# Second layer of a two-layer diffusion backbone: values scaled by one factor from norm bounds, gate loads spread over the score units, order fitted anew

## The chip, the cores and the metric

The kernel runs on one core of a Trainium2 chip. The metric is the device time of one execution in microseconds, as the median of several runs. The engines are TensorE (PE; its weight loads are listed as PEld), VectorE (DVE), ScalarE (ACT), GpSimd (POOL) and SyncE (SP), whose queue issues nearly all DMAs here.

## The reference

512 latent tokens and 256 context tokens of width 1024 pass through two layers: differential attention, then grouped-query attention (8 query heads, 2 key/value heads of width 128). Only the second layer's latent output is returned, and its context tokens are needed for keys and values alone.

```
shift, scale, gate = adaln(c, ada_w[i], ada_b[i])          # silu(c) @ w + b, split in three
h = rms_norm(x, pre_g[i]) * (1.0 + scale) + shift
...
q, k, v, z = jnp.split(p, [...], axis=-1)                  # p = h @ w_in
q = rms_norm(q, qk_g[0]); k = rms_norm(k, qk_g[1])         # then rotary positions on latent tokens
...
p = jax.nn.softmax(s, axis=-1)
o = einsum(p, v)
y = (o * silu(z)) @ w_out[i]
x = x + gate * rms_norm(y, post_g[i])
```

All inputs are float32.

## The kernel before, in words

**Precision.** A float32 product is made of three matmuls on split operands (a high part and the rest): hi*hi, hi*lo, lo*hi. Weights are loaded into a two-buffer tile `raw`, cast on ACT to `whi` (L240) and subtracted on DVE or POOL to `wlo` (L234). The class `WStream` does this in a fixed order as its slots come free.

**Second layer.** After the first layer's output projection the second layer's input `h1` is made, 256 tokens at a time, by `h1_tr` (L1342 on): transposes on TensorE, four scalings with shift per call (L1353; the first `HFD` of the four on DVE, the others on ACT; `HFD` is 4) and a split. Then comes the key/value stage: the list `KV` orders six projections (`k`, tokens m), the last two `h1_tr` calls (`t`) and the key transposes (`c`). Each projection fills a PSUM bank with 256 columns of keys and 256 of values. PSUM has four such banks in rotation (`trp` takes one briefly, `pj` holds one until `close`) and two double banks for scores.

**Values before.** Each value tile is copied to `vr` (L1450). When all six are there, they are squared to bf16 (L1457), summed over tokens on TensorE with a matrix of ones (L1459), and `col_scale` (L247 on) makes of each column's sum a power of two: Ln, Exp, and a mask on the exponent bits. Two transposes (L1465) and `col_back` make the factors that undo the scale. Then the values are multiplied by their columns' factors (L1469), cast to fp16 (L1470), and the rest is subtracted (L1471): `vp`, high and low.

**Score units.** 32 steps, four per head with 128 queries each (`s1_units`): scores, row maximum, Exp, reciprocal, a scaled copy to fp16 (`fp`, L258) and its rest (L1563). A DMA transpose on the SP queue (`turn`, L245) writes them to `ft`. Per half head (two units) 18 fp16 matmuls (`pv1_steps`, `pv_f16`, L179) multiply `ft` by the values.

**The gate.** The second layer's gate vector is computed on DVE from 512 KB slices of `ada_w`: `gate1_load` (L1601) loads a slice into `gw` (two buffers), `gate1_part` adds two products (L1614, L1616). After four slices `gate1_finish` sums over the partitions on TensorE (`colsum`), and adds the bias and multiplies by the post-norm gain (L1626, L1628). These two rows are loaded in `gate1_finish` itself, broadcast to all partitions (256 KB each), into the weight stream's `raw` tile (L1624, L1625). Loads go out after score units 1 to 8, and the two halves are finished after units 9 and 14 (`GFIN`).

**What sets the order.** `flow` is a planner: each step has a cost, lags behind other steps and a due time on a model clock. It emits the due step or, where none is due, a piece of filler work (`FILL1`: query and gate projections). `TS` spaces the score units, `LA` and `LT` are the lags of value matmuls behind scores, `SLAG1`, `QLAG` and `QTR` are other lags, `HOT1` and one row of `JT` per head are priorities and offsets. A scheduler then orders each engine's queue by these priorities.

**Near the end** `last_half` (L1630 on) multiplies the last head by its SiLU gate on the engine named by `EGL`; `subln_last` does the same in the first layer.

Of the kernel before, what the change touches and what calls it, by code (L numbers as in the profile page):

```python
# [9 lines left out]
F32 = mybir.dt.float32  # L10
# [24 lines left out]
ATT = 15.15  # L35
ACCN = (0, 1, 2, 2, 4, 0, 5, 4)
ACD = 0.71
FILL1 = (('q', 1), ('z', 2), ('z', 0), ('q', 2), ('q', 3), ('z', 1), ('z', 4), ('z', 5), ('z', 3), ('z', 6), ('z', 7))
HOT0 = (4643, 2452, 770, 3759)
HOT1 = (1948, 4101, 2904, 5806, 2112, 918)  # L40
WARM = 2019
AGB = 10
PRE = 19.12
TS = 8.22
HFD = 4
KVE = (0, 0, 1, 0)
KV = (('t', 1), ('k', 0), ('k', 2), ('k', 1), ('t', 0), ('c', 1), ('k', 3), ('c', 0), ('k', 4), ('c', 3), ('c', 2), ('k', 5))
SPL = 4.55
GAP0 = 7.06
DL0 = (0.86, 0.0, 0.73, 2.42, 2.07, 3.84, -1.78, 5.34)  # L50
# [2 lines left out]
NWARM = 16  # L53
XLATE = 1
WX = (1, 1)
LA = (9.42, 7.7)
LT = (1.27, 1.09)
AHEAD = 3
SLAG = (4.63, 0.61)
SLAG1 = 2.73  # L60
AT1 = 7.65
EGL = 'p'
EXS = 'pvvvvv'
EHF = ('vvvvvvpv', 'pvvvvvvv')
EHL = ('vvvvvvvv', 'pppppppp')
# [15 lines left out]
EG1 = 'a'  # L81
EGA = "v"
RL = 4.34
LM = (4.63, 10.96)
AB = 3
FTB = 6
JT = (((-0.86, -0.75, -0.84, -18, -0.26, 0.57), (0.1, -0.44, 0.02, 160, 0.11, -1.79), (0.07, -0.16, -0.26, -299, 1.1, 0.1), (-0.21, 0.31, -1.04, 23, 0.94, 0.71), (-0.21, -0.39, 0.3, 92, 2.85, -0.8), (-0.63, -0.11, 0.88, 16, -0.68, -3.71), (2.06, -0.05, 1.19, 296, -2.27, -0.21), (-0.02, 0.45, 1.73, -49, -0.48, 0.83)), ((-3.15, 0.21, -0.44, -128, 2.28, 0.65), (1.34, -0.8, -0.13, -164, 0, 0.55), (-2.3, -0.59, -1.0, -170, -0.88, -0.01), (0.16, -0.46, 0, -31, -0.58, -0.59), (0.54, -0.33, 0.91, 452, -1.34, -0.68), (0.65, -0.93, -2.71, 0, -0.85, -0.67), (0, -0.48, -0.44, 1330, 0, -1.3), (-0.03, 0.1, -1.26, -97, -0.6, 0.06)))


def f32(ap):  # L90
# [4 lines left out]
def tile_backbone(  # L95
# [90 lines left out]
    nc.vector.tensor_copy(ones_r, ones)  # L186
    eps = con.tile([P, 1], F32, name="eps")
    nc.vector.memset(eps, EPS)
    tiny = con.tile([P, 2], F32, name="tiny")
    nc.vector.memset(tiny[:, 0:1], 1e-30)  # L190
    nc.vector.memset(tiny[:, 1:2], 14.0 * math.log(2.0))
    mhalf = con.tile([P, 2], F32, name="mhalf")
    nc.vector.memset(mhalf, -0.5)

# [49 lines left out]
    def turn(dst, src):  # L244
        nc.sync.dma_start(dst, src, transpose=True)  # L245

    def col_scale(c, ss):  # L247
        nc.scalar.activation(c, ss, AF.Ln, bias=tiny[:, 0:1])  # L248
        nc.scalar.activation(c, c, AF.Exp, scale=-0.5, bias=tiny[:, 1:2])
        nc.vector.tensor_scalar(c.bitcast(I32), c.bitcast(I32), EXPO, None, ALU.bitwise_and)  # L250
# [1124 lines left out]
    with tc.tile_pool(name="t1", bufs=1, side="right") as t1p:  # L1375
# [7 lines left out]

        kh = t1p.tile([P, 2, T], F32R, name="kh")
        kl = t1p.tile([P, 2, T], F32R, name="kl")
        vr = t1p.tile([P, NT, 256], F32, name="vr")
        vp = t1p.tile([P, 2, NT, 256], F16, name="vp")
        vback = t1p.tile([P, 2], F32, name="vback")
        ones_b = t1p.tile([P, P], BF, name="ones_b")
        nc.vector.tensor_copy(ones_b, ones)  # L1390

        def rope_tok(dst, src, t):
            n = 2
# [44 lines left out]

        for what, m in KV:
            if what == "t":  # L1440
                hot(h1_tr, 2, m)
            elif what == "c":
                k_tr(*ktr.pop(0))
            else:
                o = pj(512)
                run(proj_tok(o, wkv, m))
                if late:
                    k_rope(*late.pop())
                late.append((m, o, head_rstd(o)))
                nc.scalar.copy(vr[:, m, :], o[:, 256:])  # L1450
        k_rope(*late.pop())
        while ktr:
            k_tr(*ktr.pop(0))
        vsq = vp[:, 1].bitcast(BF)
        ss = pj(256)
        for a in (0, 3):
            nc.scalar.activation(vsq[:, a:a + 3], vr[:, a:a + 3], AF.Square)  # L1457
        for m in range(NT):
            nc.tensor.matmul(ss, ones_b, vsq[:, m, :], start=m == 0, stop=m == NT - 1)  # L1459
        vc = t1p.tile([P, 256], F32, tag="qt", name=nm("vc"), bufs=9)  # L1460
        col_scale(vc, ss)
        close(ss)
        tr = trp()
        for g in range(2):
            nc.tensor.transpose(tr[:, g * P:(g + 1) * P], vc[:, g * P:(g + 1) * P], ident)  # L1465
        col_back(vback, tr[:, 0:256:P], 2.0 ** -16)
        for a in (0, 3):
            v = vr[:, a:a + 3]
            nc.vector.tensor_tensor(v, v, vc.unsqueeze(1).to_broadcast([P, 3, 256]), ALU.mult)  # L1469
            nc.scalar.copy(vp[:, 0, a:a + 3], v)  # L1470
            nc.vector.tensor_tensor(vp[:, 1, a:a + 3], v, vp[:, 0, a:a + 3], ALU.subtract)  # L1471
# [66 lines left out]
        def s1_units(h, ms):  # L1538
            res = []

            def unit(m):
                g = h // 4
                qa, qb = qT[h]
                sl = slice(m * P, (m + 1) * P)
                sc = sc2()
                for j in range(2):
                    c = slice(j * 384, j * 384 + 384)
                    mm3(sc[:, j, :384], qa[:, sl], qb[:, sl], kh[:, g, c], kl[:, g, c], True, True)
                scv = sc[:, :, :384]
# [7 lines left out]
                nc.scalar.activation(pt.rearrange("p (j n) -> p j n", j=2), scv, AF.Exp, scale=sr, bias=nmx, accum_out=l)
                nc.vector.reciprocal(l, l)
                nc.vector.tensor_scalar(l, l, 32768.0, None, ALU.mult)
                fp = t1q.tile([P, 3, 2, 256], F16, tag="fp", name=nm("fp"), bufs=3)  # L1560
                pv_ = pt.rearrange("p (j n) -> p j n", j=3)
                scaled(EN1, fp[:, :, 0, :], pv_, l)
                nc.vector.scalar_tensor_tensor(fp[:, :, 1, :], pv_, l, fp[:, :, 0, :], ALU.mult, ALU.subtract)  # L1563
                e = m % 2
                if e == 0:
                    res.append(t1q.tile([P, 12, 256], F16, tag="ft", name=nm("ft"), bufs=FTB // 3))
                turn(res[0][:, :, e * P:e * P + P], fp.rearrange("p j a b -> p (j a b)"))

            return res, [Step(lambda m=m: unit(m), 0.97) for m in ms]

        def pv1_steps(h, at, ch, after, ms):
# [3 lines left out]
            def mstep(i):  # L1575
# [4 lines left out]
                if i == 2:  # L1580
                    if ch == 0:
                        gT1[h] = t1p.tile([P, 512], F32, tag="g1", name=nm("g1"), bufs=8)
                    scaled(EG1, gT1[h][:, ch * 256:ch * 256 + 256], o, vback[:, g:g + 1])
                    close(o)
                    if ch == 1 and h < KT - 1:
                        done1.add(h)
                        gate_mul1(h)
                    elif ch == 1:
                        last_half(1)
# [25 lines left out]
                    else:  # L1615
                        nc.vector.scalar_tensor_tensor(acc, gs, scol[:, 0, kt:kt + 1], acc, ALU.mult, ALU.add)  # L1616

        def gate1_finish(half):
            acc = gate1[:, half * 512:half * 512 + 512]
            o = pj(512)  # L1620
            colsum(o, acc, [t1q.tile([P, 512], F32R, tag=t, name=nm("ac"), bufs=1) for t in ("za", "ac")])
            b = wp.tile([P, 1024], F32, tag="raw", name=nm("raw"), bufs=2)
            sl = slice(half * 512, half * 512 + 512)
            nc.sync.dma_start(b[:, :512], ada_b[1, 2 * D + half * 512:2 * D + half * 512 + 512].partition_broadcast(P))  # L1624
            nc.sync.dma_start(b[:, 512:], post_g[1, sl].partition_broadcast(P))  # L1625
# [50 lines left out]
        for h in range(KT):  # L1676
# [5 lines left out]
            for ch in range(2):  # L1682
# [9 lines left out]
                if h == KT - 1 and ch == 1:  # L1692
                    T_.append(Step(tail1, 0.0, [(M_[-1], 0.0), (u[-1], 0.0)]))
                pv1_steps(h, at, ch, u[-1], M_)
        Y_ = [Step(lambda i=i: gate1_finish(i), 0.9, [(S_[GFIN[i]], 0.0)], hot=False) for i in range(2)]
        Z_ = []
        for i in range(8):
            if i >= 0:
                Z_.append(Step(lambda i=i: gate1_load(i // 4, i % 4), 0.0, [(S_[1 + i], 0.0)], hot=False))
            if i:  # L1700
                Z_.append(Step(lambda i=i: gate1_part((i - 1) // 4, (i - 1) % 4), 0.0, [(S_[1 + i + 1], 0.0)], hot=False))
        Z_.append(Step(lambda: gate1_part(1, 3), 0.0, [(S_[1 + 9], 0.0)], hot=False))
        flow(1, [S_, T_, M_, X_, Z_, Y_])
# [153 lines left out]
```

## Time and profile before

| | us |
|---|---|
| median of 3 runs (lowest, highest) | 774.57 (774.52, 774.81) |
| the profiled execution's own time | 775.77 |
| its span in the profile | 774.0 |
| PE busy | 751.9 |
| DVE, ACT, POOL busy | 527.0, 454.4, 286.6 |

The profile lists busy time of each engine, groups of equal instructions by source line, and for each idle stretch of an engine what ended it (the releaser). A row such as `bk<-ft,vp` names the tile written and the tiles read. `SPq` rows are DMAs issued by SP; their duration is that of the issue, and the time to landing is given apart. The second layer's input is made from about 500 us on; the key/value stage ends near 553 us, the score units run from about 580 to 728, and the last output projection ends at 767.9.

### The profile page before, as it was taken

The numbers are of one execution on the slowest core, as the hardware profiler recorded it, in microseconds if no ns is written. First come the engines' busy times: TensorE is split into PE (matmuls) and PEld (weight loads), VectorE is DVE, ScalarE is ACT, GpSimd is POOL, SyncE is SP. The second block draws the span as 40 slices with busy tenths as digits, with TensorE's granted clock in tenths as the row PEclk, the third lists the DMA queues.
The fourth block names the chain that finished last, engine by engine and source line by source line (L and its number), as shares of the span: only waits on it lengthen the run. The fifth ranks groups of instructions, "written<-read, shape, count | busy, mean of one in ns | idle before, by whom it ended". The sixth has DMA issues, their size and how long they took to land. (4 is left out here: it accounts for less than half of the span.)

```text
span 774.0 us, 13084 instructions
## 1 busy us (share of the span) xinstructions
PE 751.9 (97%) x4884; PEld 649.7 (84%) x4884; DVE 527.0 (68%) x962; ACT 454.4 (59%) x952; POOL 286.6 (37%) x386
## 2 busy tenths in 40 slices
PE   8999999999999999999999999999899869999996
PEld 6788888889998989888988888888799869888885
DVE  4766666677676766757776825498667886877724
ACT  5546464575575564575577834364558646987822
POOL 0010455664335543355425411466261524322201
PEclk9999999999999999999999999999999989999998
DMA  9924311330332233222142006031326894756602
GB/s 343 396 81 168 109 55 42 124 96 28 96 96 82 70 109 124 69 96 96 58 170 101 28 1 244 29 111 60 110 82 164 191 218 110 159 141 136 164 1 108
DMA packets 83215, 90.28 MB, mean 117 GB/s; under 512 B 53584, under 2 KB 56144, under 8 KB 83152
## 3 DMA queue, kind: packets, MB, share of 16 engines
q1 hardware_dynamic: 79296, 83.64, 36.3%
q10 hardware_dynamic: 3856, 5.81, 2.0%
q8 instruction: 38, 0.62, 0.3%
q14 instruction: 25, 0.20, 0.1%
HBM read 70.56 MB, written 2.10 MB: 94 GB/s over the span
## 5 line engine op out<-in xcount | busy, mean ns | idle before, releaser
L162 PE MATMUL bk<-h,whi 128*128 128x512 f32 (+2 forms) x864 | 228.1, 347 | 0.5 <-DVE al L1062 0.5
L162 PE MATMUL bk<-whi,h 128*128 128x256 f32 (+1 forms) x928 | 213.2, 318 | 3.0 <-ACT vc L248 1.6
L162 PEld LDWEIGHTS bk<-whi,h 128*128 128x128 f32 x928 | 154.7, 189 | 19.0 <-issue 3.7
L162 PEld LDWEIGHTS bk<-h,whi 128*128 128x128 f32 x864 | 150.4, 188 | 18.6 <-issue 2.4
L162 PE MATMUL bk<-h,wlo 128*128 128x512 f32 (+2 forms) x432 | 148.3, 345 | 0.0
L162 PE MATMUL bk<-wlo,h 128*128 128x256 f32 (+1 forms) x464 | 146.4, 318 | 0.0
L234 DVE TENSOR_TENSOR wlo<-raw,whi 128x1024 fp32r<-128x1024 f32 (+2 forms) x70 | 83.3, 1193 | 34.3 <-ACT whi L240 34.1
L162 PEld LDWEIGHTS bk<-wlo,h 128*128 128x128 f32 x464 | 87.3, 189 | 7.6 <-issue 1.3
L162 PEld LDWEIGHTS bk<-h,wlo 128*128 128x128 f32 x432 | 81.3, 188 | 7.8 <-issue 1.1
L240 ACT CAST whi<-raw 128x1024 fp32r<-128x1024 f32 x64 | 67.2, 1049 | 33.3 <-PE bk L162 17.6
L234 POOL TENSOR_TENSOR sz<-sz,za 128x192 f32<-128x192 f32 (+1 forms) x48 | 34.8, 746 | 118.4 <-ACT za L214 118.4
L1001 ACT ACTIVATE p<-sc,sm 128x768 f32<-128x768 f32 (+1 forms) x68 | 59.6, 878 | 28.5 <-DVE sm L998 28.2
L260 POOL TENSOR_SCALAR p<-p,sm 128x768 f32<-128x768 f32 (+1 forms) x48 | 39.7, 831 | 97.1 <-DVE sm L1004 78.2
L998 DVE TENSOR_REDUCE sm<-sc 128x1 f32<-128x768 f32 (+1 forms) x68 | 61.1, 918 | 15.8 <-PE sc L993 15.7
L1061 ACT CAST ah<-bk 128x512 fp32r<-128x512 f32 x56 | 31.9, 588 | 36.5 <-PE bk L1058 33.9
L1062 DVE TENSOR_TENSOR al<-bk,ah 128x512 fp32r<-128x512 f32 x56 | 37.9, 686 | 22.5 <-ACT ah L1061 22.1
L993 PE MATMUL sc<-qk,qk 64*128 64x384 f32 (+1 forms) x396 | 43.8, 351 | 0.1
L179 PE MATMUL bk<-ft,vp 128*128 128x256 f16 x288 | 36.6, 282 | 7.3 <-DMA ft<-fp 7.1
L1009 DVE SCALAR_TENSOR_TENSOR p<-p,sm,p 128x768 f32<-128x768 f32 (+1 forms) x34 | 37.0, 1087 | 9.1 <-POOL p L260 6.9
L162 PE MATMUL sc<-whi,h 128*128 128x512 f32 x128 | 42.0, 396 | 0.0
L179 PEld LDWEIGHTS <-vp 128*128 128x128 f16 x288 | 27.8, 101 | 14.6 <-DMA ft<-fp 6.1
L234 POOL TENSOR_TENSOR qk<-qr,qk 128x256 fp32r<-128x256 f32 x42 | 31.5, 786 | 21.5 <-ACT qk L888 16.3
(249 smaller groups left out, 1415.3 us busy)
## 6 DMA issues: line engine op xcount, KB each, us to landing
raw<-in_a_w SPq DMA_DIRECT2D x28, 512.0 KB, 3.4
araw<-in_ada_w SPq DMA_DIRECT2D x12, 1024.0 KB, 5.0
raw<-in_b_w SPq DMA_DIRECT2D x20, 512.0 KB, 3.5
ag<-in_ada SPq DMA_DIRECT2D x16, 512.0 KB, 7.7
raw<-in_w_out SPq DMA_DIRECT2D x16, 512.0 KB, 3.7
sw<-qr ACTq DMA_DIRECT2D x32, 128.0 KB, 2.1
gw<-in_ada_w SPq DMA_DIRECT2D x8, 512.0 KB, 4.1
xnt<-in_xlT SPq DMA_DIRECT2D x4, 512.0 KB, 5.8
```

The costliest lines, as they stand in the source:

```text
L162: i = nc.tensor.matmul(o, a, b, start=start, stop=stop)
L179: nc.tensor.matmul(o, v[:, a, kt + e, c], f[:, 2 * b + e, :], start=first and i == 0, stop=last and i == 5)
L234: eng.tensor_tensor(dst[:, i:i + n], a[:, i:i + n], b[:, i:i + n], op)
L240: nc.scalar.copy(hi, r)
L260: (nc.vector if eng == "v" else nc.gpsimd).tensor_scalar(dst, src, s_, 1.0, ALU.mult, ALU.mult)
L993: prev = nc.tensor.matmul(sc[m][:, j if nk == T else m, :w], a[r, tok], b[r, c], start=i == 0, stop=i == 2)
L998: nc.vector.tensor_reduce(mx, scv, AX.XY if nk == T else AX.X, ALU.max, negate=True)
L1001: nc.scalar.activation(pv_, scv, AF.Exp, bias=mx, accum_out=l[:, m:m + 1])
L1009: nc.vector.scalar_tensor_tensor(ps_[0], pt, r, ps_[0], ALU.mult, ALU.add)
L1061: nc.scalar.copy(ah, tr)
L1062: nc.vector.tensor_tensor(al, tr, f32(ah), ALU.subtract)
```

## The change

Seven edits:

1. One factor for all values takes the place of one per column. `h_bound` sums the squares of the second layer's shift and scale vectors, `v_scale` sums the squares of the value columns of the four weight tiles, and the two sums bound the norm of every value. From the bound one power of two is made before the first projection, and `v_split` writes each value tile from PSUM straight to its two fp16 parts. The squares, the column sums, the transposes and the multiplications behind the stage are gone. The factor that undoes the scale is the same for both heads.
2. The gate's steps are one chain: step i is due after score unit int(2.08 + 2.79 i), i = 0 to 10. A step handles the slice loaded by the step before and loads the next. The two rows are loaded by a step of their own (`gate1_rows`) into a `gw` buffer, one step ahead of `gate1_finish`.
3. `HFD` goes from 4 to 2, so that two of the four scalings in `h1_tr` run on ACT.
4. `KVE`: of the four key/value weight tiles the first, and not the third, has its `wlo` made on POOL.
5. `EGL` goes from POOL to DVE.
6. `KV` and `FILL1` have another order.
7. The planner's numbers are others, in the second layer alone.

```
-FILL1 = (('q', 1), ('z', 2), ('z', 0), ('q', 2), ('q', 3), ('z', 1), ('z', 4), ('z', 5), ('z', 3), ('z', 6), ('z', 7))
+FILL1 = (('q', 1), ('z', 2), ('z', 0), ('q', 2), ('q', 3), ('z', 1), ('z', 3), ('z', 4), ('z', 6), ('z', 5), ('z', 7))
-HOT1 = (1948, 4101, 2904, 5806, 2112, 918)
+HOT1 = (2169, 4095, 3201, 5846, 2552, 918)
-TS = 8.22
-HFD = 4
-KVE = (0, 0, 1, 0)
-KV = (('t', 1), ('k', 0), ('k', 2), ('k', 1), ('t', 0), ('c', 1), ('k', 3), ('c', 0), ('k', 4), ('c', 3), ('c', 2), ('k', 5))
+TS = 8.25
+HFD = 2
+KVE = (1, 0, 0, 0)
+KV = (('k', 0), ('t', 1), ('k', 2), ('k', 1), ('t', 0), ('c', 1), ('k', 3), ('c', 0), ('k', 4), ('c', 2), ('c', 3), ('k', 5))
-LA = (9.42, 7.7)
-LT = (1.27, 1.09)
+LA = (9.42, 7.03)
+LT = (1.27, 1.11)
-SLAG1 = 2.73
+SLAG1 = 2.79
-EGL = 'p'
+EGL = 'v'
-GFIN = (9, 14)
+GD = (2.08, 2.79)
-QTR = 10.07
+QTR = 9.95
...
+    def norm_sum(cols, n):
+        o = trp()[:, 0:1]
+        for i in range(n):
+            nc.tensor.matmul(o, ones, cols[:, i:i + 1], start=i == 0, stop=i == n - 1)
+        return o
+
+    def h_bound(layer):
+        t = con.tile([P, 4], F32, tag="vcol", name=nm("hb"), bufs=3)
+        for which, k in ((0, 2.0), (1, 2.0 * D)):
+            jk = trp()[:, :2 * KT].rearrange("p (v k) -> p v k", v=2)
+            nc.scalar.activation(jk, mods[:, layer, :, which, :], AF.Square, scale=k ** 0.5, accum_out=t[:, which:which + 1])
+        nc.vector.tensor_copy(hb2[:, layer:layer + 1], norm_sum(t, 2))
+
+    def v_scale(layer, ws_, junk, k):
+        n = len(ws_)
+        t = con.tile([P, 4], F32, tag="vcol", name=nm("vn"), bufs=3)
+        for i, w in enumerate(ws_):
+            nc.scalar.activation(junk(), f32(w), AF.Square, accum_out=t[:, i:i + 1])
+        c = con.tile([P, 4], F32, tag="vcol", name=nm("vc"), bufs=3)
+        nc.scalar.activation(c[:, 0:1], norm_sum(t, n), AF.Ln, scale=hb2[:, layer:layer + 1], bias=tiny[:, 0:1])
+        nc.scalar.activation(c[:, 0:1], c[:, 0:1], AF.Exp, scale=-0.5, bias=tiny[:, 1:2])
+        nc.vector.tensor_scalar(c[:, 0:1].bitcast(I32), c[:, 0:1].bitcast(I32), EXPO, None, ALU.bitwise_and)
+        col_back(c[:, 1:2], c[:, 0:1], k)
+        return c
+
+    def v_split(vp, t, o, c):
+        nc.scalar.activation(vp[:, 0, t], o, AF.Copy, scale=c[:, 0:1])
+        nc.vector.scalar_tensor_tensor(vp[:, 1, t], o, c[:, 0:1], vp[:, 0, t], ALU.mult, ALU.subtract)
...
         wkv = [ws.get(i) for i in (8, 9, 10, 11)]
         late, ktr = [], []
+        h_bound(1)
+        vc = v_scale(1, [w[0].rearrange("p (k n) -> p k n", k=2)[:, :, 256:] for w in wkv], lambda: h1p.tile([P, 2, 256], BF, tag="vj", name=nm("vj"), bufs=1), 2.0 ** -16)
...
-                nc.scalar.copy(vr[:, m, :], o[:, 256:])
+                v_split(vp, m, o[:, 256:], vc)
...
-        for a in (0, 3):
-            nc.scalar.activation(vsq[:, a:a + 3], vr[:, a:a + 3], AF.Square)
-        for m in range(NT):
-            nc.tensor.matmul(ss, ones_b, vsq[:, m, :], start=m == 0, stop=m == NT - 1)
-        vc = t1p.tile([P, 256], F32, tag="qt", name=nm("vc"), bufs=9)
-        col_scale(vc, ss)
-        close(ss)
...
-            nc.vector.tensor_tensor(v, v, vc.unsqueeze(1).to_broadcast([P, 3, 256]), ALU.mult)
-            nc.scalar.copy(vp[:, 0, a:a + 3], v)
-            nc.vector.tensor_tensor(vp[:, 1, a:a + 3], v, vp[:, 0, a:a + 3], ALU.subtract)
...
-                    scaled(EG1, gT1[h][:, ch * 256:ch * 256 + 256], o, vback[:, g:g + 1])
+                    scaled(EG1, gT1[h][:, ch * 256:ch * 256 + 256], o, vc[:, 1:2])
...
+        def gate1_rows(half):
+            b = gws[half, 4] = t1q.tile([P, 1024], F32, tag="gw", name=nm("gb"), bufs=2)
             sl = slice(half * 512, half * 512 + 512)
             nc.sync.dma_start(b[:, :512], ada_b[1, 2 * D + half * 512:2 * D + half * 512 + 512].partition_broadcast(P))
             nc.sync.dma_start(b[:, 512:], post_g[1, sl].partition_broadcast(P))
...
-        Y_ = [Step(lambda i=i: gate1_finish(i), 0.9, [(S_[GFIN[i]], 0.0)], hot=False) for i in range(2)]
         Z_ = []
-        for i in range(8):
-            if i >= 0:
-                Z_.append(Step(lambda i=i: gate1_load(i // 4, i % 4), 0.0, [(S_[1 + i], 0.0)], hot=False))
+        for i in range(11):
+            late_ = [(S_[int(GD[0] + GD[1] * i)], 0.0)]
             if i:
-                Z_.append(Step(lambda i=i: gate1_part((i - 1) // 4, (i - 1) % 4), 0.0, [(S_[1 + i + 1], 0.0)], hot=False))
-        Z_.append(Step(lambda: gate1_part(1, 3), 0.0, [(S_[1 + 9], 0.0)], hot=False))
-        flow(1, [S_, T_, M_, X_, Z_, Y_])
+                f, cost = (gate1_finish, 0.9) if i % 5 == 0 else (lambda half, i=i: gate1_part(half, (i - 1) % 5), 0.0)
+                Z_.append(Step(lambda i=i, f=f: f((i - 1) // 5), cost, late_, hot=False))
+            if i < 10:
+                f = gate1_rows if i % 5 == 4 else lambda half, i=i: gate1_load(half, i % 5)
+                Z_.append(Step(lambda i=i, f=f: f(i // 5), 0.0, late_, hot=False))
+        flow(1, [S_, T_, M_, X_, Z_])
```

Of `JT` only the second layer's eight rows differ.

More of the change, by code (lines that the diff above doesn't have):

```diff
@@ L83 @@
 RL = 4.34
-LM = (4.63, 10.96)
+LM = (4.63, 10.94)
 AB = 3
-FTB = 6
-JT = (((-0.86, -0.75, -0.84, -18, -0.26, 0.57), (0.1, -0.44, 0.02, 160, 0.11, -1.79), (0.07, -0.16, -0.26, -299, 1.1, 0.1), (-0.21, 0.31, -1.04, 23, 0.94, 0.71), (-0.21, -0.39, 0.3, 92, 2.85, -0.8), (-0.63, -0.11, 0.88, 16, -0.68, -3.71), (2.06, -0.05, 1.19, 296, -2.27, -0.21), (-0.02, 0.45, 1.73, -49, -0.48, 0.83)), ((-3.15, 0.21, -0.44, -128, 2.28, 0.65), (1.34, -0.8, -0.13, -164, 0, 0.55), (-2.3, -0.59, -1.0, -170, -0.88, -0.01), (0.16, -0.46, 0, -31, -0.58, -0.59), (0.54, -0.33, 0.91, 452, -1.34, -0.68), (0.65, -0.93, -2.71, 0, -0.85, -0.67), (0, -0.48, -0.44, 1330, 0, -1.3), (-0.03, 0.1, -1.26, -97, -0.6, 0.06)))
+JT = (((-0.86, -0.75, -0.84, -18, -0.26, 0.57), (0.1, -0.44, 0.02, 160, 0.11, -1.79), (0.07, -0.16, -0.26, -299, 1.1, 0.1), (-0.21, 0.31, -1.04, 23, 0.94, 0.71), (-0.21, -0.39, 0.3, 92, 2.85, -0.8), (-0.63, -0.11, 0.88, 16, -0.68, -3.71), (2.06, -0.05, 1.19, 296, -2.27, -0.21), (-0.02, 0.45, 1.73, -49, -0.48, 0.83)), ((-3.15, 0.21, -0.44, -128, 2.28, 0.69), (1.27, -0.8, -0.1, 65, -0.08, 1.07), (-2.3, -0.84, -1.14, 69, -0.88, 0), (1.25, 0.04, 0, 721, -0.58, -0.62), (0.58, -0.04, 0.52, 604, 0.04, 0.06), (0.41, -0.95, -2.95, 60, -1.31, -1.14), (0.75, -0.49, -1.4, 1427, 0, -1.44), (0.04, 0.48, -1.17, 217, 1.04, 0.15)))
 def f32(ap):
@@ L188, in tile_backbone @@
     nc.vector.memset(eps, EPS)
-    tiny = con.tile([P, 2], F32, name="tiny")
+    consts = con.tile([P, 8], F32, name="consts")
+    tiny, psc, hb2 = (consts[:, i:i + 2] for i in (0, 2, 4))
     nc.vector.memset(tiny[:, 0:1], 1e-30)
-    nc.vector.memset(tiny[:, 1:2], 14.0 * math.log(2.0))
+    nc.vector.memset(tiny[:, 1:2], 15.0 * math.log(2.0))
     mhalf = con.tile([P, 2], F32, name="mhalf")
@@ L245, in turn @@
         nc.sync.dma_start(dst, src, transpose=True)
[L247 to L250, printed above, removed]
+    def norm_sum(cols, n):
[23 more added lines that the diff above has]
+        nc.vector.scalar_tensor_tensor(vp[:, 1, t], o, c[:, 0:1], vp[:, 0, t], ALU.mult, ALU.subtract)
     def col_back(d, tr, k):
@@ L1385, in tile_backbone @@
         kl = t1p.tile([P, 2, T], F32R, name="kl")
-        vr = t1p.tile([P, NT, 256], F32, name="vr")
         vp = t1p.tile([P, 2, NT, 256], F16, name="vp")
-        vback = t1p.tile([P, 2], F32, name="vback")
-        ones_b = t1p.tile([P, P], BF, name="ones_b")
-        nc.vector.tensor_copy(ones_b, ones)
         def rope_tok(dst, src, t):
@@ L1453, in tile_backbone @@
             k_tr(*ktr.pop(0))
-        vsq = vp[:, 1].bitcast(BF)
-        ss = pj(256)
-        for a in (0, 3):
-            nc.scalar.activation(vsq[:, a:a + 3], vr[:, a:a + 3], AF.Square)
-        for m in range(NT):
-            nc.tensor.matmul(ss, ones_b, vsq[:, m, :], start=m == 0, stop=m == NT - 1)
-        vc = t1p.tile([P, 256], F32, tag="qt", name=nm("vc"), bufs=9)
-        col_scale(vc, ss)
-        close(ss)
[L1463 to L1471, printed above, removed]
         ws.release(8, 9, 10, 11, retract=True)
@@ L1565, in unit @@
                 if e == 0:
-                    res.append(t1q.tile([P, 12, 256], F16, tag="ft", name=nm("ft"), bufs=FTB // 3))
+                    res.append(t1q.tile([P, 12, 256], F16, tag="ft", name=nm("ft"), bufs=2))
                 turn(res[0][:, :, e * P:e * P + P], fp.rearrange("p j a b -> p (j a b)"))
@@ L1616, in gate1_part @@
                         nc.vector.scalar_tensor_tensor(acc, gs, scol[:, 0, kt:kt + 1], acc, ALU.mult, ALU.add)
[L1618 to L1622, printed above, removed]
+        def gate1_rows(half):
+            b = gws[half, 4] = t1q.tile([P, 1024], F32, tag="gw", name=nm("gb"), bufs=2)
             sl = slice(half * 512, half * 512 + 512)
@@ L1625, in gate1_finish @@
             nc.sync.dma_start(b[:, 512:], post_g[1, sl].partition_broadcast(P))
+        def gate1_finish(half):
+            acc = gate1[:, half * 512:half * 512 + 512]
+            b = gws.pop((half, 4))
+            o = pj(512)
+            colsum(o, acc, [t1q.tile([P, 512], F32R, tag=t, name=nm("ac"), bufs=1) for t in ("za", "ac")])
             nc.vector.tensor_tensor(acc, o, b[:, :512], ALU.add)
```

## The prediction

> **What bounds the kernel now.** First the page: the span, the engine shares, and the slices in which TensorE (PE) is not full.
>
> ```profile
> span 774.0 us, 13084 instructions
> PE 751.9 (97%) x4884; PEld 649.7 (84%) x4884; DVE 527.0 (68%) x962; ACT 454.4 (59%) x952; POOL 286.6 (37%) x386
> PE   8999999999999999999999999999899869999996
> PEclk9999999999999999999999999999999989999998
> DMA  9924311330332233222142006031326894756602
> ```
>
> PE is the bound: it idles 774.0 - 751.9 = 22.1 us in all. A change that leaves PE's work alone can win only from this idle time and from work done at a low clock. The slices (19.35 us each) say where: the first and last, which this change leaves alone, one at 542 to 561 us (an 8), and 600 to 639 (8 and 6), where the granted clock dips too and the DMA engines are at 8 and 9 tenths. Next the busy times by stretch (its length, then busy us of PE, PEld, DVE, ACT and POOL, each with its instructions; granted clock, DMA share, GB/s), then PE's own waits from 490 us on (total, times, longest).
>
> ```profile
> 480.00:520.00 40.00, 40.00 (x192) 32.79 (x191) 26.50 (x38) 18.07 (x42) 20.70 (x36) 1.00 0.23 73
> 520.00:560.00 40.00, 37.43 (x217) 32.12 (x215) 31.41 (x66) 20.95 (x61) 16.92 (x26) 1.00 0.30 96
> 600.00:640.00 40.00, 32.24 (x228) 28.92 (x228) 33.53 (x73) 21.55 (x50) 14.05 (x18) 0.92 0.93 197
> 640.00:680.00 40.00, 38.36 (x259) 34.63 (x258) 32.12 (x68) 32.16 (x62) 13.90 (x18) 1.00 0.62 145
> 680.00:720.00 40.00, 39.87 (x227) 33.89 (x225) 28.36 (x53) 32.37 (x53) 12.05 (x16) 1.00 0.63 138
> PE bk L179 <- DMA ft<-fp: 7.1, 3, 5.2
> PE sc L162 <- ACT p L1557: 1.8, 2, 1.2
> PE bk L162 <- ACT vc L248: 1.6, 1, 1.6
> PE bk L162 <- DVE kl L1424: 1.0, 1, 1.0
> ```
>
> These four waits are 11.5 us of the 22.1, all in the second layer. The 1.6 and the 1.0 are the column scale of the values (L248) and the end of the key/value stage; the 7.1 is TensorE waiting for transposed probabilities (`ft`) that a DMA must turn. In order of time they are single gaps:
>
> ```profile
> 546.90 0.49 PE L1459 MATMUL bk<-vp,ones_b 128*128 128x256 bf16 x3
> 548.35 0.39 PE L162 MATMUL bk<-whi,h 128*128 128x256 f32 x1 [0.96 <-DVE kl L1424]
> 553.65 0.39 PE L162 MATMUL bk<-whi,h 128*128 128x256 f32 x1 [1.61 <-ACT vc L248]
> 557.36 0.38 PE L1465 MATMUL bk<-ident,vc 128*128 128x128 f32 x2
> 608.88 2.13 PE L179 MATMUL bk<-ft,vp 128*128 128x256 f16 x18 [0.29 <-DMA ft<-fp]
> 612.92 0.35 PE L162 MATMUL bk<-whi,h 128*128 128x256 f32 x1 [0.42 <-DVE tb L1399]
> 618.77 0.44 PE L162 MATMUL sc<-kh,qh 128*128 128x384 f32 x1 [1.24 <-ACT p L1557]
> 629.45 0.44 PE L162 MATMUL sc<-kh,qh 128*128 128x384 f32 x1 [0.59 <-ACT p L1557]
> 636.00 4.02 PE L179 MATMUL bk<-ft,vp 128*128 128x256 f16 x18 [5.22 <-DMA ft<-fp]
> 678.12 2.12 PE L179 MATMUL bk<-ft,vp 128*128 128x256 f16 x18 [1.64 <-DMA ft<-fp]
> ```
>
> The long gap costs more than its 5.22 us: the same 18 matmuls take 4.02 us behind it and 2.13 elsewhere, 1.89 more. What made that one transpose late stands in the SyncE queue (SP) just before it, with the landing times of all 32 transposes in the last row:
>
> ```profile
> 623.80 0.34 SPq L1624 DMA_DIRECT2D raw<-in_ada_b  x1
> 624.19 0.43 SPq L1625 DMA_DIRECT2D raw<-in_post_g  x1
> 624.94 0.33 SPq L238 DMA_DIRECT2D raw<-in_b_w  x1
> 625.66 0.38 SPq L1601 DMA_DIRECT2D gw<-in_ada_w  x1
> 627.52 2.68 SPq L245 DMA_TRANSPOSE ft<-fp  x1
> DMA to landing us min/median/max: 3.2/3.4/8.4
> ```
>
> Four loads (256, 256, 512 and 512 KB, 1.5 MB) were issued within 1.9 us, and the transpose behind them landed at 636, after 8.4 us instead of 3.4. Three of the four belong to the second layer's gate: two rows (bias, post-norm gain) and a weight slice. All three are what the change spreads.
>
> **The change, part by part.** *Values.* It removes, at the end of the key/value stage, six bf16 matmuls (L1459: 0.11 us apart, (0.49 - 0.27)/2, where 0.27 is what a lone one takes), two transposes (taken at 0.11), and a chain through ACT and DVE:
>
> ```profile
> L1469 DVE TENSOR_TENSOR vr<-vr,vc 128x768 f32<-128x768 f32 x2 | 2.4, 1228 | 0.0
> L1471 DVE TENSOR_TENSOR vp<-vr,vp 128x768 f16<-128x768 f32 x2 | 1.9, 946 | 0.0
> L1457 ACT ACTIVATE vp<-vr 128x768 bf16<-128x768 f32 x2 | 1.7, 856 | 0.0
> L1470 ACT CAST vp<-vr 128x768 f16<-128x768 f32 x2 | 1.7, 832 | 2.4 <-DVE vr L1469 2.4
> L1450 ACT COPY vr<-bk 128x256 f32<-128x256 f32 x6 | 2.2, 371 | 0.0
> L258 ACT ACTIVATE g<-bk,vback 128x256 f32<-128x256 f32 x16 | 7.5, 469 | 15.3 <-PE bk L179 15.3
> L1424 DVE TENSOR_TENSOR kl<-bk,kh 128x256 fp32r<-128x256 f32 x6 | 2.4, 420 | 2.2 <-ACT kh L1423 2.2
> L1295 ACT ACTIVATE jk<-x 128x512 bf16<-128x512 f32 x4 | 2.5, 631 | 3.1 <-issue 3.1
> ```
>
> That is 4.3 us of DVE (2.4 + 1.9) and 5.6 of ACT (1.7 + 1.7 + 2.2). It adds, per token tile, one scaled ACT copy (nearest row 0.469) and one DVE subtract from PSUM (nearest 0.420): 2.8 and 2.5 us. It also adds four ACT squares of 128x512 (0.63 each and about 0.2 for reading the sum: 3.3 us) and some one-column operations. ACT rises by about 1 us, DVE falls by 1.8. Both have room: ACT is busy 18 of 40 us in 480:520 and 21 in 520:560. PE waits for neither as long as the factor is there when the first value tile is evacuated.
>
> What the waits were: at 553.65 PE wanted the PSUM bank that the column sum held until L248. That bank is not taken any more, so 1.61 goes. At 548.35 it wanted a bank behind the last key transpose; two bank users fewer make this earlier, but the key chain itself stays. I take 0.6 of the 0.96 as gone (bounds 0 and 0.96). On PE 8 x 0.11 = 0.9 us of matmuls goes; six matmuls of one column come, between 0 and 0.11 each, since a transpose of 128 columns takes 0.11; I take 0.3 for all six. Sum: 1.6 + 0.6 + 0.9 - 0.3 = 2.8 us. The new price on PE's path: the six small matmuls wait for ACT's squares, and TensorE runs in order. Here the bound is 0 (squares done, since the last weight cast comes several us before the first key/value tile is ready) to 3.3 us (all four squares waited for). I take 0, because ACT is half idle there.
>
> *Gate.* The same loads, products and sums, but one step about every 2.79 score units instead of every unit: the steps run from unit 2 to unit 29 instead of 1 to 14, and the two rows load one step ahead of their use, into the gate's own buffers and not into the weight stream's. So the three gate loads of 623.8 to 625.7 no longer meet. The stall of 5.22 goes with its 1.89 of slow clock: 7.1 us. If the weight load alone stays in front of that transpose, the nearest row is 678.12, where a transpose landed after 5.0 us and PE waited 1.64; that is the upper bound of what remains.
>
> The Trainium skill (TensorE: Matmul & The Clock Gate, Part 1) says that the clock falls to half after an idle window of about 3.4 us. The trace agrees: the granted clock stays 1.00 in 640:680 with its gap of 1.64, and the 18 matmuls behind 5.22 take 4.02/2.13 = 1.9 times as long. By that rule a remainder below 3.4 us carries no clock loss at all; shared out in proportion, a remainder of 1.64 would carry 0.6 more.
>
> The crowded stretch also has DVE at 33.5 of 40 us, with gate products between the score units. Behind it lie the gaps 0.29 + 0.42 + 1.24 + 0.59 = 2.5 us. Each gate slice is two products of 0.75 us:
>
> ```profile
> L1616 DVE SCALAR_TENSOR_TENSOR gate<-gw,scol,gate 128x512 f32<-128x512 f32 x14 | 10.6, 759 | 1.7 <-DMA gw<-in_ada_w 1.7
> L1353 DVE TENSOR_SCALAR hf<-sc,mods 128x256 f32<-128x256 f32 x24 | 11.4, 538 | 0.7 <-PE sc L1347 0.4
> ```
>
> About half of these 10.6 us move behind 640, where DVE has 8 to 12 us free in 40. I take half of the 2.5 as won, 1.3 (bounds 0 and 2.5).
>
> What the moved loads do later: 2 MB of products and 0.5 MB of rows for the second half now fall between about 640 and 720, where the DMA share is 0.62 and the transposes go on. The gap at 678.12 shows the price of meeting one: 1.64. I leave that gap as it is and add one more of its size, -1.6 (bounds 0 and three of them, 4.9; below nothing only if the gap at 678 goes as well, +1.6). SP runs in order, so a gate load also stands ahead of a transpose in its queue, but its issue takes only 0.4 us.
>
> The Trainium skill (DMA: Bandwidth & Descriptors, Where 436 GB/s comes from) puts the ceiling at 435 GB/s; by it 1.5 MB ahead would delay a transpose by an estimated 3.6 us. The trace shows 8.4 - 3.4 = 5.0, so the queue behind a load is worse here than by the page; by the page's rate the new waits would be 1.2 us each and the sum 0.4 better.
>
> *Other edits.* Twelve of the 24 scalings of the second layer's input (L1353) go from DVE to ACT: -6.5 us of DVE, +5.6 (12 x 0.469) of ACT, in 500 to 535, where PE waits for neither; nothing. The split of one key/value weight tile on POOL is another tile now, in a stretch where POOL idles; nothing. The last product with the SiLU gate goes from POOL to DVE in both layers, under matmuls that run without a gap; nothing. The order of the fills and the planner's lags move work on an engine that is otherwise full: the score-to-value lag shrinks by 0.67 planner us, so transposes have less time. That is in the -1.6.
>
> **Sum.** 2.8 + 7.1 + 1.3 - 1.6 = 9.6 us off a span of 774.0: 764.4. The profiled execution took 775.77, 1.77 more than its span; the median of the runs is 774.57, 0.57 above the span. So 765.0. Own range: at best 2.8 + 0.4 + 7.1 + 2.5 + 1.6 = 14.4, that is 760.2; at worst 2.8 - 0.6 (the key chain's wait stays) - 1.7 (half of the squares are waited for) + 7.1 - 1.6 + 0 - 4.9 = 1.1, that is 773.5.
>
> **Rivals.** Two times within 0.2% (1.5 us) are what a measurement here can't tell apart.
> *The stall moves.* A gate load, a weight load and a transpose meet at another place once, and PE idles over 5 us there with the slow clock again. For it: the DMA share is already over 0.6 to 720, and the lag is shorter. Against: only one of 32 transposes landed after 8.4 us, and it took four loads at once. Then 7.1 is lost again: 764.4 + 7.1 = 771.5, 772.1 as a median.
> *Slower.* The place is 640 to 720: the second half's loads meet the output weights' loads and the pairs of transposes there, with the shorter lag, twice in the way of 636. Each costs 7.1; two of them 14.2 against 9.6 won: 778.6, 779.2 as a median. It decides as soon as new waits on `ft`, their slow clock included, pass 9.6 + 1.6 = 11.2 us. For it: a single weight load made 1.64 there. Against: loads that were one per 4 us are one per 11.
> *No change.* The new order gives back in small PSUM and score-bank waits (like 1.24 and 0.59) what the gaps gave: 773 to 776. Against: all four kinds of gap lose their cause.
>
> **How the numbers follow.** Forecast 0.70; the stall moves 0.12 (faster too); no change 0.06; slower 0.12. So faster 0.82, same 0.06, slower 0.12. The range from 760.2 to 774.0 holds the forecast, the moved stall and half of no change.
>
> **What would show it.** Right: no more than 0.5 us of PE idle where the key/value stage ends (546 to 554 before); no gap over 3.4 us on `ft`, the longest landing of a transpose near 5; granted clock 1.00 in 600:640; PE busy 749 to 751 of a span near 764. Wrong: waits on `ft` in 640:720 above 5 us in sum; PE waiting for an ACT square before the first key/value tile; DVE over 90% in a stretch behind 640 with PE waiting for it.

## The result, and the profile after

| | before | after |
|---|---|---|
| median us | 774.69 | 765.42 (765.35 to 765.54) |
| span of the profiled execution | 774.0 | 763.6 |
| PE busy | 751.9 | 751.3 |
| PE idle | 22.1 | 12.3 |

The ratio is 0.988, with a 95% interval of 0.9863 to 0.9897: 9.3 us faster. 765.0 was forecast. (The 774.69 is the median of four runs; three of them gave the 774.57 above.)

The page of the changed kernel, the same lines as before. All `L` numbers are those of its own source: L161 and L178 are the matmul helpers that were L162 and L179, L1561 is the Exp of a score unit (L1557 before).

```profile
span 763.6 us, 13109 instructions
PE 751.3 (98%) x4888; PEld 651.9 (85%) x4888; DVE 519.4 (68%) x956; ACT 460.1 (60%) x972; POOL 288.3 (38%) x382
PE   8999999999999999999999999999999999999996
PEclk9999999999999999999999999999999999999999
DMA  9925311320223143114044104212335798876503
```

The 8 at the end of the key/value stage and the 8 and 6 of the old stall are gone, and so is the dip of the clock there. DVE fell by 7.6 us and ACT rose by 5.7. The busy times by stretch show where PE idles now:

```profile
520.00:560.00 40.00, 40.00 (x238) 35.04 (x237) 28.51 (x66) 22.09 (x70) 19.32 (x30) 1.00 0.28 89
600.00:640.00 40.00, 39.87 (x312) 38.06 (x312) 34.91 (x78) 29.18 (x68) 20.08 (x27) 1.00 0.81 166
640.00:680.00 40.00, 40.00 (x240) 34.73 (x238) 33.09 (x66) 32.03 (x58) 10.60 (x12) 1.00 0.82 196
680.00:720.00 40.00, 37.68 (x201) 31.33 (x200) 33.18 (x58) 32.87 (x55) 12.32 (x14) 0.96 0.62 139
```

600:640 was 32.24 of 40 and is 39.87. The DMA share there fell from 0.93 to 0.81, and in 640:680 it rose from 0.62 to 0.82: these are the moved gate loads, and no gap of PE is put down to one of them. Of all PE gaps behind 480 us one is left that has a releaser, and it is new; then the landing times of the 32 transposes:

```profile
707.47 0.50 PE L161 MATMUL sc<-whi,h 128*128 128x512 f32 x1 [2.32 <-ACT p L1561]
DMA to landing us min/median/max: 3.6/4.0/4.8
```

The longest landing is 4.8 us where it was 8.4, but the median rose from 3.4 to 4.0. Both the new gap and the higher median are followed below.

The balance of the span: the eight gaps listed in the prediction (0.96 + 1.61 + 0.29 + 0.42 + 1.24 + 0.59 + 5.22 + 1.64) are gone, -12.0 us; the new one is +2.3; PE's busy time is 0.6 less. That makes -10.3 of the measured -10.4. Among the eight is the 1.64 at 678.12, which the prediction had left standing.

### The profile page after: what moved, and what is told of

Its sections match the earlier page's. It is cut to its first block, busy times and chain, and to the rows that moved or that the text cites. A ratio compares the mean times of both kernels' runs of the same rounds, so it can differ in the third digit from the quotient of the medians.

```text
span 763.6 us, 13109 instructions
## 1 busy us (share of the span) xinstructions
PE 751.3 (98%) x4888; PEld 651.9 (85%) x4888; DVE 519.4 (68%) x956; ACT 460.1 (60%) x972; POOL 288.3 (38%) x382
## 4 chain that ended last, share of the span: by engine, by line
PE 89%; DMA 5%; ACT 2%; DVE 2%; issue 1%; POOL 1%; ACTq 0%; SPq 0%; DVEq 0%; POOLq 0%
PE bk L161 56%; PE sc L161 12%; PE bk L173 5%; PE sc L1017 5%; PE bk L178 4%; PE bk L1082 3%; DMA ag<-in_ada 2%; PE bk L858 1%; DMA xnt<-in_xlT 1%; PE sc L1046 1%; PE sc L1371 1%; DMA ft<-fp 1%; DMA raw<-in_w_out 1%; PE bk L460 1%; DMA sw<-qr 1%
## 5 line engine op out<-in xcount | busy, mean ns | idle before, releaser
L161 PE MATMUL bk<-h,whi 128*128 128x512 f32 (+2 forms) x864 | 228.4, 347 | 0.2 <-DVE al L1086 0.2
L161 PE MATMUL bk<-whi,h 128*128 128x256 f32 (+1 forms) x928 | 214.0, 319 | 0.0
L161 PEld LDWEIGHTS bk<-whi,h 128*128 128x128 f32 x928 | 155.1, 189 | 15.1 <-issue 3.1
L161 PEld LDWEIGHTS bk<-h,whi 128*128 128x128 f32 x864 | 150.8, 188 | 18.2 <-issue 2.4
L161 PE MATMUL bk<-h,wlo 128*128 128x512 f32 (+2 forms) x432 | 148.7, 345 | 0.0
L161 PE MATMUL bk<-wlo,h 128*128 128x256 f32 (+1 forms) x464 | 147.0, 319 | 0.0
L161 PEld LDWEIGHTS bk<-wlo,h 128*128 128x128 f32 x464 | 87.4, 189 | 7.5 <-issue 1.3
L161 PEld LDWEIGHTS bk<-h,wlo 128*128 128x128 f32 x432 | 81.3, 188 | 7.8 <-issue 1.1
L161 PE MATMUL sc<-whi,h 128*128 128x512 f32 x128 | 43.4, 407 | 2.3 <-ACT p L1561 2.3
L1017 PEld LDWEIGHTS sc<-qk,qk 64*128 64x128 f32 x396 | 32.9, 184 | 7.6 <-issue 3.0
L1561 ACT ACTIVATE p<-sc,sm,qrs 128x768 f32<-128x768 f32 x32 | 31.7, 990 | 9.0 <-DVE sm L1558 5.7
```

The source lines that it names most:

```text
L161: i = nc.tensor.matmul(o, a, b, start=start, stop=stop)
L1017: prev = nc.tensor.matmul(sc[m][:, j if nk == T else m, :w], a[r, tok], b[r, c], start=i == 0, stop=i == 2)
```

## The experiments

The theory was the prediction's: the gate's spread removes the stall, the values' edit removes two waits, the order is neutral. The rival called 'order' says that the fitted order makes the gain; the rival called 'any shift' says that whatever moves the score stage by some us removes the stall. The diff was cut into three parts that can be taken alone: **values** (one factor, split from PSUM), **gate** (chain of steps, rows in `gw`), **order** (fills, `KV`, planner's numbers, `HFD`, `KVE`, `EGL`). Each run is compared with the kernel before on the same chip, on which that kernel took 774.99 to 776.38 us; the row of the whole change in the next table is the result above, against 774.69.

### The parts alone and in pairs

Gate alone:

```
-            b = wp.tile([P, 1024], F32, tag="raw", name=nm("raw"), bufs=2)
+            b = gws.pop((half, 4))          # loaded one step ahead by gate1_rows
...
+            late_ = [(S_[int(GD[0] + GD[1] * i)], 0.0)]
```

> The kernel before with the gate's edit alone (loads and rows spread over the score units; values and order as before). Theory (the loads met in front of one transpose): the gap of 5.2 us on ft and its slow clock go, the two waits at the end of the key/value stage (1.0 and 1.6) stay: 766 to 769 us. Rival 'order' (the gain is the fitted order's): 773 to 776, the gap stays or another one over 3 us takes its place.

Values alone:

```
-                nc.scalar.copy(vr[:, m, :], o[:, 256:])
+                v_split(vp, m, o[:, 256:], vc)
```

> The kernel before with the values' edit alone (one factor, split from PSUM). Theory: the two waits at the end of the key/value stage go, the gap of about 5 us on ft stays: 771 to 772.5 us. Rival 'order': no more than 1 us, 773.5 to 775. Rival 'any shift' (whatever moves the score stage by a few us takes the loads and the transpose apart): the gap on ft goes too, 764 to 767.

Order alone:

```
-LA = (9.42, 7.7)
+LA = (9.42, 7.03)
...
-HFD = 4
+HFD = 2
```

> The kernel before with the other edits alone (fills, key/value order, planner's lags and offsets, HFD, KVE, EGL); the values and the gate as before. Theory: both waits at the end of the key/value stage stay and a gap over 3 us on ft stays or moves: 773 to 777 us. Rival 'order': at least two thirds of the gain, 768 us or less.

Values and gate, with the order of before:

> Both the values' and the gate's edit, with the order and the planner's numbers of before. Theory: the gains of the two add up, 764 to 767 us, and the refitted order is worth under 2 us. Rival 'order': without the new order the two edits give less than half of the gain, 770 us or more.

Gate and order, with the values of before:

> The changed kernel with the values done as before (column scale behind the stage); gate and order as changed. Theory: two waits of about 1.0 and 1.6 us at the end of the key/value stage come back, with 0.9 us of matmuls: 767.5 to 769.5 us. Rival 'order': 765 to 766.5.

Values and order, with the gate of before:

> The changed kernel with the gate's loads as before (one per unit, rows loaded in the weight stream's buffer where they are used); values and order as changed. Theory: a gap of over 3 us on ft with a slow clock comes back: 770 to 774 us. Rival 'any shift': no such gap, 765 to 767.

| parts | median us | ratio to before | interval |
|---|---|---|---|
| values | 774.38 | 0.9985 | 0.9975 to 0.9994 |
| gate | 769.44 | 0.9916 | 0.9899 to 0.9933 |
| order | 783.15 | 1.0098 | 1.0082 to 1.0114 |
| values, gate | 769.11 | 0.9911 | 0.9890 to 0.9931 |
| gate, order | 768.56 | 0.9896 | 0.9873 to 0.9918 |
| values, order | 779.92 | 1.0054 | 1.0037 to 1.0071 |
| all (the changed kernel) | 765.42 | 0.9880 | 0.9863 to 0.9897 |

The gate's part makes most of the gain. Alone it gives 0.84%, 6.5 us by that ratio and 6.0 by the medians; the two kernels with the new order and the old gate are slower than before. The rival 'order' falls: the new order alone costs 7.7 us. 'Any shift' falls too: in the values' run and in the two with the new order and the old gate, the long gap on `ft` is still there. Here it is in each of the three (values; order; values and order):

```profile
635.76 2.53 PE L179 MATMUL bk<-ft,vp 128*128 128x256 f16 x11 [4.95 <-DMA ft<-fp]
```
```profile
632.22 0.44 PE L161 MATMUL sc<-kh,qh 128*128 128x384 f32 x1 [2.18 <-ACT p L1556]
639.70 4.00 PE L178 MATMUL bk<-ft,vp 128*128 128x256 f16 x18 [6.12 <-DMA ft<-fp]
721.85 0.44 PE L161 MATMUL sc<-kh,qh 128*128 128x384 f32 x1 [1.56 <-ACT p L1556]
725.13 0.50 PE L161 MATMUL sc<-whi,h 128*128 128x512 f32 x1 [1.97 <-ACT p L1556]
```
```profile
636.62 1.65 PE L178 MATMUL bk<-ft,vp 128*128 128x256 f16 x7 [4.21 <-DMA ft<-fp]
```

In the order's run the list shows what the new order does without the gate's spread: the gap on `ft` is longer than before (6.12 against 5.22), and there are new waits for a score bank (2.18, 1.56, 1.97). With the gate spread no gap that long is left in either order, but only in the new order are the waits on `ft` gone: there is none in the changed kernel, and one of 0.33 us with gate and order. In the old order value matmuls still wait about 2 us twice. With both edits the gaps are 2.59 and 2.15 us (the two lines stand in the last section). With the gate alone they are 2.09 us at 629.94, which the profile puts down to DVE, and 1.58 us at 713.84. The view of `ft` in that run has them (total, times):

```profile
its engine sat idle before it (us, times) until:
  DVE sm L1558: 2.1, 1
  DMA ft<-fp: 1.6, 1
```

Behind the first of these the granted clock is 0.50 from 631 to 633 us, so the gate's part alone does not take away every stall with a slow clock. What the new order does once the loads are spread can be read from these lists: it removes the two waits (4.7 us in the kernel with values and gate) and brings the one of 2.32 us at 707.

The values' edit removes its waits and yet gains little. The start of the value matmuls against the kernel before, in the values' run:

```profile
592.23 2.14 PE L179 MATMUL bk<-ft,vp 128*128 128x256 f16 x18 [0.33 <-DMA ft<-fp]
608.76 2.13 PE L179 MATMUL bk<-ft,vp 128*128 128x256 f16 x18 [1.38 <-DMA ft<-fp]
618.65 0.44 PE L162 MATMUL sc<-kh,qh 128*128 128x384 f32 x1 [1.89 <-ACT p L1562]
```

No gap with a releaser is left between 470 and 592, so 2.57 us of waits are gone. But the group that began at 608.88 before begins at 608.76. Up to there 1.4 us of the lead are lost in longer waits for transposes (0.33 and 1.38 where there was one of 0.29), and the next wait for a score bank is 1.89 where it was 1.24. Where the rest went was not followed; PE is busy for 754.2 us in this run against 751.9 before. That the transposes and the softmax chain limit the stage behind fits these waits, but is not shown by a run. Added to the gate's spread in the old order, the values' edit gives nothing that can be measured (769.11 against 769.44). In the new order with the old gate it gives 3.2 us (779.92 against 783.15), with intervals that do not overlap. There the old values cost more than in the old order, since the new order opens a third wait behind the keys; with gate and order it is the first of these:

```profile
536.54 0.50 PE L161 MATMUL bk<-whi,h 128*128 128x512 f32 x1 [1.48 <-DVE kl L1423]
549.65 0.39 PE L161 MATMUL bk<-whi,h 128*128 128x256 f32 x1 [0.83 <-DVE kl L1423]
555.02 0.38 PE L161 MATMUL bk<-whi,h 128*128 128x256 f32 x1 [1.69 <-ACT vc L247]
```

The values' edit takes these 4.0 us away: from gate and order to the whole change the profiled span falls by 3.4 us (767.0 to 763.6), though the intervals of the two ratios overlap.

Of the six expectations above, only that for gate and order was met by its theory (768.56 in 767.5 to 769.5). The gate alone came out just above its range (769.44 against 766 to 769). The values alone came out at 774.38, where the rival 'order' had that run (773.5 to 775). The two kernels with the new order and the old gate were slower than their theories allowed. And the gains of values and gate did not add up to 764 to 767: in the old order they came to 769.11.

### Which loads held up the transpose

The kernel before without the two row loads (so the second layer's gate lacks its bias and post-norm gain):

```
-            nc.sync.dma_start(b[:, :512], ada_b[1, ...].partition_broadcast(P))
-            nc.sync.dma_start(b[:, 512:], post_g[1, sl].partition_broadcast(P))
+            nc.gpsimd.memset(b, 1.0)
```

> The kernel before without the loads of the gate's two rows (the second layer's gate is computed with ones in the place of bias and post-norm gain; a GpSimd memset fills them). Of the 1.5 MB in front of the late transpose 0.5 MB are missing. Theory (the transpose waits for the bytes queued ahead, about 1.6 us for each 0.5 MB): it lands after 6.5 to 7 us instead of 8.4, PE waits 3 to 4 us instead of 5.2: 771.5 to 773.5 us. Rival (the rows are small beside the weight slices): the gap stays above 4.7 us, 774 to 775.

769.97 us, ratio 0.9928 (0.9914 to 0.9943). Both expectations were too high. The gap did not shrink by a third; 0.59 of its 5.22 us is left, and that the profile puts down to DVE:

```profile
631.23 2.13 PE L179 MATMUL bk<-ft,vp 128*128 128x256 f16 x18 [0.59 <-DVE fp L1563]
```

So the long gap needs the rows: without their half a megabyte no wait for that DMA is left. Whether it also needs the gate slice was not tried, since no run leaves out the slice and keeps the rows. What the rows do is seen in the landing of the weight load and the slice that went out behind them (620 to 640 us, the kernel before; then 622 to 637, without the rows):

```profile
raw<-in_b_w SPq DMA_DIRECT2D x1, 512.0 KB, 6.7
gw<-in_ada_w SPq DMA_DIRECT2D x1, 512.0 KB, 7.3
```
```profile
raw<-in_b_w SPq DMA_DIRECT2D x1, 512.0 KB, 3.4
gw<-in_ada_w SPq DMA_DIRECT2D x1, 512.0 KB, 4.1
```

The two rows, each 256 KB written from a row of 2 KB, held up what stood behind them by 3.3 and 3.2 us. The estimate by bytes (1.6 us for each 0.5 MB) was half of that.

### The new gap, and a version that removes it

At 707.47 the output projection wants the first score bank. The Exp that frees it had its last operand at 701.92 (DVE's row), but ACT did five casts of gated heads and one of weights first:

```profile
701.76 0.16 DVE L1558 TENSOR_TENSOR sm<-sm,qrs 128x1 f32<-128x1 f32 x1
701.83 0.97 ACT L1561 ACTIVATE p<-sc,sm,qrs 128x768 f32<-128x768 f32 x1
702.80 2.68 ACT L1646 CAST h<-g 128x512 fp32r<-128x512 f32 x5
705.39 1.04 ACT L240 CAST whi<-raw 128x1024 fp32r<-128x1024 f32 x1
706.34 0.99 ACT L1561 ACTIVATE p<-sc,sm,qrs 128x768 f32<-128x768 f32 x1
```

Behind the gap the clock falls too (busy times by stretch; the granted clock is the third figure from the right):

```profile
704.00:708.00 4.00, 1.68 (x9) 1.31 (x9) 4.00 (x6) 4.00 (x8) 1.25 (x2) 1.00 0.00 0
708.00:712.00 4.00, 4.00 (x12) 3.16 (x11) 4.00 (x7) 3.00 (x5) 2.07 (x2) 0.60 0.11 25
```

At 0.60 in these 4 us, 1.6 us of PE's work is lost by estimate (0.40 x 4) beside the 2.3 us of idle time. The edit queues the casts behind the Exp of unit 30, and leaves the rest to the scheduler:

```
-                nc.scalar.copy(ghi[kt], gT1[kt])
+                with tc.issue_after(px1[-2].ins): nc.scalar.copy(ghi[kt], gT1[kt])   # px1: the Exps of the units
```

> The changed kernel, and on ACT the casts that split the gated heads for the output projection are queued behind the Exp of the last unit but one (in the changed kernel five of them, 2.7 us, stand ahead of it, and TensorE waits 2.3 us for that score bank at 707 us, then runs at a low clock). Theory (the new gap is this order on ACT): the gap falls under 1 us and the matmuls behind it run at full clock: 761 to 763.5 us. Rival (the output projection waits for the casts instead): a gap of 1.5 us or more on them, 764.5 to 767.

762.29 us, ratio 0.9821 (0.9801 to 0.9840). As the theory had it: two gaps of 0.43 and 0.27 us are left in the place of 2.32, at full clock.

```profile
705.93 0.50 PE L161 MATMUL sc<-whi,h 128*128 128x512 f32 x1 [0.43 <-ACT h L1646]
706.93 0.73 PE L161 MATMUL sc<-whi,h 128*128 128x512 f32 x2 [0.27 <-DVE h L1647]
```
```profile
704.00:708.00 4.00, 3.30 (x18) 2.35 (x16) 3.55 (x6) 4.00 (x9) 2.33 (x2) 1.00 0.28 84
708.00:712.00 4.00, 4.00 (x19) 3.14 (x18) 4.00 (x6) 3.51 (x6) 2.48 (x2) 1.00 0.15 54
```

### The slower landing

In the runs above with the values' edit the transposes land after 4.0 us by the median, in those without it after 3.4 or 3.5. The edit makes the constants 96 bytes per partition longer and adds a tile of 1024 bytes (`vj`, for the squares), and with them later tiles begin elsewhere: `ft` 1120 bytes further, 32 more than a multiple of 64 and 96 more than a multiple of 256. (These moves are added up from the sizes of the tiles in the sources; the profile shows no addresses.) Four kernels move the tiles and leave every instruction and its order as it is.

```
-    tiny = con.tile([P, 2], F32, name="tiny")
+    tiny = con.tile([P, 10], F32, name="tiny")         # the kernel before, 32 bytes longer
...
-    consts = con.tile([P, 8], F32, name="consts")
+    consts = con.tile([P, 16], F32, name="consts")     # the three others, moved by a multiple of 64
```

> The kernel before with one constant tile 32 bytes per partition longer, so that all later tiles (fp, ft, raw, gw) begin 32 bytes further and no longer at a multiple of 64; every engine's instructions and their order are the same. Theory (in all kernels with the values' edit the transposes land after 4.0 us instead of 3.4, because their tiles lie at 32 modulo 64): median landing 4.0, waits on ft 1 to 3 us longer, 775 to 778 us where before takes about 775 on this chip, ratio 1.001 to 1.004. Rival (the slower landing belongs to the values' edit itself): 3.4, ratio within 0.1% of 1.

> The values' edit alone (as in the run of that edit alone), with 32 bytes of padding that put the tiles back at multiples of 64; the same instructions in the same order. Theory: landing back at 3.4, waits on ft under 7.5 us, and 1 to 2.5 us of the edit's hidden gain appear: ratio to before 0.995 to 0.9975 instead of 0.9985. Rival: landing 4.0, ratio 0.998 to 0.999.

> The changed kernel with the same 32 bytes of padding; the same instructions in the same order. Theory: landing 3.4, but no time changes, since TensorE does not wait for ft in the changed kernel: ratio 0.987 to 0.989. Rival (the slow landing also holds up what the profile does not show as a wait on ft): 0.985 or less.

> The changed kernel with the tail's casts queued behind the Exp of the last unit but one, and with the padding. Theory: landing 3.4, the gap of 0.16 us on ft goes, the rest stays: ratio 0.981 to 0.983, the fastest of all. Rival: the earlier landings reorder the last units and open a gap in the tail again: 0.984 or more.

| kernel | `ft` moved against before, bytes modulo 256 | median landing us | median us | ratio (interval) |
|---|---|---|---|---|
| before, moved by 32 | 32 | 4.0 | 774.24 | 0.9989 (0.9980 to 0.9998) |
| values alone, padded | 128 | 3.9 | 775.06 | 1.0001 (0.9992 to 1.0010) |
| changed, padded | 128 | 3.9 | 765.38 | 0.9874 (0.9859 to 0.9888) |
| changed with the tail's edit, padded | 128 | 3.9 | 763.32 | 0.9847 (0.9834 to 0.9861) |

The first half of the theory holds: 32 bytes alone take the landing of the kernel before from 3.4 to 4.0 us.

```profile
DMA to landing us min/median/max: 3.7/4.0/8.2
```

The second half falls. A move by a multiple of 64 does not bring 3.4 back. In the kernels with 3.4 or 3.5 these additions leave `ft` where it was before; in all others it is moved by 32, 96 or 128 bytes modulo 256. A values' edit moved by a multiple of 256 was not tried, so this stays a correlation. And the slower landing costs no measurable time: the moved kernel is not slower than before, and the padded changed kernel takes what the changed one takes. So it is not what eats the values' gain. The times went against the theory for two of the four: 1.001 to 1.004 was expected for the moved kernel (0.9989) and 0.995 to 0.9975 for the padded values (1.0001).

The last two rows ran on the same chip and differ by the tail's edit alone: 763.32 against 765.38, 2.1 us. The last one missed its theory (0.981 to 0.983). Its ratio lies where the rival had it, yet the rival's reason did not come: no gap over 0.27 us opened in the tail again. Of the 2 us between its ratio and the one without padding (0.9821), 1.4 lie in the kernel before, which took 776.38 us in the one comparison and 774.99 in the other; the rest stays open.

## Why the prediction was right

- **The result** lies at the forecast (765.42 against 765.0), by terms that were partly off and cancelled; that it lies so close is luck.
- **The stall on `ft`** (7.1 us): right in mechanism, and nearly in size. Alone the gate's edit gives 6.0 to 6.5 us; in the changed kernel no gap on `ft` is left. Its cause was read too broadly. Three gate loads were named; without the two rows alone the long gap was gone.
- **The crowded stretch** (1.3 of 2.5): too small. All 2.5 us are gone in the changed kernel, and so is the 1.64 at 678.12, for which nothing was booked. With the gate alone 0.75 of the 2.5 stays (0.27 and 0.48).
- **The values** (2.8): the waits went as foreseen, with all of the 0.96 and not 0.6. TensorE did not wait for the squares, as assumed. The six small matmuls were booked at 0.3; they stand as twelve instructions in the trace, busy for 0.50 + 0.73 + 0.28 = 1.5 us. Above all, the term was booked as if the next stage took up the lead, and that holds only in some orders: 1.1 us alone, nothing measurable beside the gate's spread in the old order, 3.2 us in the new order with the old gate.
- **New waits** (-1.6): one of that size does come on `ft` behind 640 when the gate is spread in the old order (1.58 at 713.84 with the gate alone, 2.15 at 711.62 with the values too). In the changed kernel there is none, although the DMA share rose to 0.82. There the wait came at the start of the output projection, on ACT's order, at 2.3 us and a low clock. Taking it away gave 2.1 us with the padded tiles and 4.6 without, by the ratios (0.9880 to 0.9821).
- **The order** (nothing, with its shorter lag put into the -1.6): the step that failed most. Alone it costs 7.7 us. With both other parts it is worth 2.4 us by the ratios (0.9911 to 0.9880; the intervals overlap) and 3.5 by the profiled spans (767.1 to 763.6). Without the loads spread it loses. With them spread the gap lists show what it does: two waits of 2.59 and 2.15 us go and one of 2.32 comes. Which of its numbers does this was not taken apart and stays open.
- **The rivals**: the moved stall and the stall in 640 to 720 did not come. Of 'no change' one part came, a new wait for a score bank (2.32), but it gave back only a small part of the gain. The clock rule's consequence, no loss behind a gap under 3.4 us, was not borne out.

## What to carry to other kernels

When PE waits for a DMA, list what was issued in the few us ahead of it, and leave out one load at a time (here this was done for the rows only): the small broadcast rows did here what their bytes did not suggest. A wait removed ahead of a stage that waits for something else can reappear there; follow the start times of the next groups to see whether the lead lasts. An order fitted to one set of transfers can be a loss with another, so test the edit and the order apart; and look at each engine's queue where one stage hands over to the next, for work that stands ahead of the instruction that frees the buffer.

## What was not expected of the hardware

- **Gaps of about 2 us can halve the clock.** Behind the gap of 2.32 us in the changed kernel the granted clock was 0.60 on average from 708 to 712, and 0.50 from 709.5 to 711.5. The Trainium skill (TensorE: Matmul & The Clock Gate, Part 1) speaks of an idle window of about 3.4 us. A gap shorter than that was enough here, but not always. In the values-and-gate run a gap of 2.59 us at 628.79 left the clock at 1.00, and one of 2.15 at 711.62 brought the 18 matmuls behind it to 3.53 us instead of 2.14:

```profile
628.79 1.49 PE L179 MATMUL bk<-ft,vp 128*128 128x256 f16 x12 [2.59 <-DMA ft<-fp]
711.62 3.53 PE L179 MATMUL bk<-ft,vp 128*128 128x256 f16 x18 [2.15 <-DMA ft<-fp]
```

  So the length of a gap alone did not decide; what else does was not tested.
- **Two broadcast rows of 256 KB each** held up the loads behind them by 3.3 and 3.2 us (6.7 and 7.3 us to landing, against 3.4 and 4.1 without them).
- **32 bytes of tile address** change the median landing of a DMA transpose from 3.4 to 4.0 us with the same instructions in the same order.
